# First-layer tiles of two squared-ReLU MLPs: pairs by quarters in seven products for eight, weights' sums on GpSimd

## Chip, cores and metric

The kernel runs on one core of one Trainium2 chip. The metric is the device time of one execution in microseconds (us). Before the change the median of three runs is 1992.46 us (1991.14 to 1993.85).

## What is computed

The input is x, 512 tokens by 1024 features, in float32. Two blocks follow each other: the first (latent attention beside a gated convolution, a gated feed-forward network, a gated embedding) and the second, which does this twice:

```python
for i in range(DEPTH_2):                       # DEPTH_2 = 2
    hn = _rmsnorm(h, mix_norm_g[i])
    h = h + (_retention if i % 2 == 0 else _chunk_attention)(hn, ...)
    h = h + _sqrelu_mlp(_rmsnorm(h, mlp_norm_g[i]), mlp_w1[i], mlp_w2[i])
return _rmsnorm(h, final_norm_g)

def _sqrelu_mlp(h, w1, w2):                    # w1: 1024 x 4096, w2: 4096 x 1024
    u = jax.nn.relu(h @ w1)
    return (u * u) @ w2
```

The change lies in `h @ w1` of the two MLPs, called MLP0 and MLP1 below.

## The kernel before

**Precision.** Every float32 operand of a product is split into a high part of TensorE's reduced float32 type and a low part, the rest. A product of a 128x128 weight tile with 128x512 activations is three matmuls into one bank of PSUM: high by high, low by high, high by low (`mm3`, L165 to L168). Activations lie features by tokens: eight `hn` pairs (`pair()`: high and low, 128x512 each) hold the normed input without the row factor, which the norm's spread `norm.r` brings in after the product.

**Weights.** `weights()` fetches one row of 128x128 tiles as a raw tile `wr` of 128x1024 (512 KB, one DMA on SyncE's queue, SP, L152; three buffers), ScalarE copies it to the high part `wh` (L129), VectorE subtracts to the low part `wl` (L113). Copy and subtraction are given a priority of 80 steps ahead (`HW`).

**An MLP** (`mlp`, from L969) goes in four groups. Each group has eight first-layer tiles (128 of the 4096 hidden features; eight tiles of depth by three matmuls are 24 matmuls of 512 columns), each followed by `square_relu`: VectorE multiplies the bank by `norm.r` (L107), takes max(t,0)*t (L975), and the split into a hidden pair follows (ScalarE L129, VectorE L113). Then come eight second-layer tiles (`m_w2`), each eight hidden pairs deep, which VectorE adds to the residual `xs` (L110). In group 0 the first two tiles are interleaved while the norm is being finished.

**Order.** TensorE's instructions run in the order in which the code writes them (`manual_schedule`, with generators that yield between pieces of a product). The order on the other engines' queues is set by a scheduler from the program and the priorities. Every queue runs in order: an instruction that waits holds up all behind it. Pools: 22 pairs, 8 temporaries of 128x512 (`tmp`), 8 banks of PSUM.

Of the kernel before, what the change touches and what calls it, by code (L numbers as in the profile page):

```python
# [7 lines left out]
F32 = mybir.dt.float32  # L8
# [6 lines left out]
P = 128  # L15
T = 512
# [45 lines left out]
def kernel(  # L62
# [32 lines left out]
    def f32(ap):  # L95
        return ap.bitcast(F32)
# [871 lines left out]

    def mlp(i, now, nxt):  # L969
        norm, hn = now.norm, now.hn  # L970

        def square_relu(hid, ps):
            t = tmp()
            mul(t, ps, norm.r)
            dve.scalar_tensor_tensor(out=t, in0=t, scalar=0.0, in1=t, op0=ALU.max, op1=ALU.mult)  # L975
            pr = pair()
            split(pr, t)
            hid.append(pr)

        def group(hid, grp):  # L980
            if grp == 0:

                two = [(bank(), weights(rows(m_w1, i * 32 + j))) for j in range(2)]
                yield from together([units(ps, w, K8, hn) for ps, w in two],
                                    [lambda ps=ps: norm.then(lambda: square_relu(hid, ps)) for ps, _ in two])
            for j in range(2 if grp == 0 else 0, 8):
                w = weights(rows(m_w1, i * 32 + grp * 8 + j))
                ps = bank()
                yield from units(ps, w, K8, hn)
                norm.then(lambda ps=ps: square_relu(hid, ps))  # L990
                yield

        for grp in range(4):
            hid = []
            gen = group(hid, grp)
# [4 lines left out]
            for mt in range(KT - 3 if ends else KT):  # L1000
# [432 lines left out]
```

## Time and profile before

| | |
|---|---|
| median of 3 runs | 1992.46 us (1991.14 to 1993.85) |
| the profiled execution, its own time | 1992.6 us |
| its span in the trace | 1990.8 us, 23850 instructions |
| TensorE matmuls (PE) busy | 1966.9 us, 99% |
| VectorE (DVE) busy | 1188.7 us, 60% |
| ScalarE (ACT) busy | 805.9 us, 40% |
| GpSimd (POOL) busy | 9.7 us |
| DMA | 185.31 MB, mean 93 GB/s |
| first-layer tiles of group 1 of MLP0 | 1134.70 to 1178.20 us |

The profiled execution's own time is 1.8 us above its span and 0.14 us above the median. Busy times sum the modelled durations; matmuls overlap each other, so that one matmul's duration is longer than the distance from its start to the next one's start. That distance, called spacing below, is a window's length divided by the matmuls that start in it.

### The profile page before, as it was taken

Reading aid. Unit: us, or ns where it says so; the run is one execution under the profiler, and the core shown is the slowest. Engines: PE = TensorE matmul, PEld = TensorE weight load, DVE = VectorE, ACT = ScalarE, POOL = GpSimd, SP = SyncE. Lnnn points to the kernel's source line nnn. Section 1 sums busy time; section 2 is a strip of 40 time slices with the busy share of each in tenths; the row PEclk is TensorE's granted clock in tenths of the full one; section 3 lists DMA queues with packets and bytes.
Section 4 is the critical chain, followed back from the end, with each engine's and each line's share of the span. In section 5 each row is a group of like instructions: output and inputs, shape, how many; then the busy total and the mean of one; then the engine's idle time right before and its main releaser. Section 6 shows DMA issues by size and latency. Waiting matters only on the chain.

```text
span 1990.8 us, 23850 instructions
## 1 busy us (share of the span) xinstructions
PE 1966.9 (99%) x9348; PEld 1643.8 (83%) x9348; DVE 1188.7 (60%) x2106; ACT 805.9 (40%) x1301; POOL 9.7 (0%) x21
## 2 busy tenths in 40 slices
PE   9999999999999999999999999999999999999998
PEld 7787888888888888888888888888888888888887
DVE  7878963343469665536565344455598975444354
ACT  5776542222245444233443222223476753222232
POOL 1000000000000000000000000000000000000000
PEclk9999999999999999999999999999999999999999
DMA  5122223232232222222222232222222223232321
GB/s 189 63 70 82 85 85 96 98 102 96 88 120 85 100 78 77 100 91 78 76 98 94 100 100 95 96 96 95 101 85 79 70 97 106 95 98 98 101 95 64
DMA packets 59041, 185.31 MB, mean 93 GB/s; under 512 B 6928, under 2 KB 10400, under 8 KB 58928
## 3 DMA queue, kind: packets, MB, share of 16 engines
q1 hardware_dynamic: 53936, 176.02, 26.2%
q10 hardware_dynamic: 4688, 7.40, 1.2%
q8 instruction: 73, 1.20, 0.3%
q0 software_dynamic: 304, 0.36, 0.1%
q14 instruction: 40, 0.33, 0.1%
HBM read 181.56 MB, written 2.20 MB: 92 GB/s over the span
## 4 chain that ended last, share of the span: by engine, by line
PE 89%; DVE 6%; ACT 3%; issue 1%; DMA 0%; POOLq 0%; POOL 0%; ACTq 0%; DVEq 0%
PE bank L166 29%; PE bank L168 29%; PE bank L167 29%; DVE wl L113 1%; PE bank L415 1%; PE bank L396 1%; ACT tmp L383 1%; ACT pair L129 1%; DVE pair L113 1%; DVE tmp L110 1%; DVE tmp L380 1%; DVE pt L113 1%; ACT wh L129 1%; PE bank L318 0%; DVE tmp L389 0%
## 5 line engine op out<-in xcount | busy, mean ns | idle before, releaser
L166 PE MATMUL bank<-pair,wh 128*128 128x512 f32 (+1 forms) x2550 | 978.8, 384 | 0.3 <-ACT pair L129 0.3
L168 PE MATMUL bank<-pair,wh 128*128 128x512 f32 (+1 forms) x2550 | 969.6, 380 | 0.5 <-DVE pair L113 0.3
L167 PE MATMUL bank<-pair,wl 128*128 128x512 f32 (+1 forms) x2550 | 968.5, 380 | 0.0
L129 ACT ACTIVATE wh<-wr 128x1024 fp32r<-128x1024 f32 (+5 forms) x355 | 353.7, 998 | 889.7 <-PE bank L168 643.3
L168 PEld LDWEIGHTS bank<-pair,wh 128*128 128x128 f32 x2550 | 480.0, 188 | 93.1 <-DVE pair L113 1.7
L166 PEld LDWEIGHTS bank<-pair,wh 128*128 128x128 f32 x2550 | 480.4, 188 | 87.8 <-ACT pair L129 0.9
L167 PEld LDWEIGHTS bank<-pair,wl 128*128 128x128 f32 x2550 | 480.6, 188 | 87.5 <-DVE wl L113 0.8
L113 DVE TENSOR_TENSOR wl<-wr,wh 128x1024 fp32r<-128x1024 f32 (+5 forms) x355 | 405.9, 1144 | 147.6 <-ACT wh L129 146.8
L107 DVE TENSOR_TENSOR tmp<-bank,rb 128x512 f32<-128x512 f32 (+1 forms) x140 | 94.4, 678 | 239.1 <-PE bank L168 235.3
L110 DVE TENSOR_TENSOR x<-x,bank 128x512 f32<-128x512 f32 (+1 forms) x99 | 66.2, 671 | 212.0 <-PE bank L168 211.9
L129 ACT ACTIVATE pair<-tmp 128x512 fp32r<-128x512 f32 (+1 forms) x188 | 118.6, 632 | 102.9 <-DVE tmp L975 28.3
L113 DVE TENSOR_TENSOR pair<-tmp,pair 128x512 fp32r<-128x512 f32 (+1 forms) x156 | 106.8, 687 | 12.3 <-ACT pair L129 11.3
L166 PE MATMUL bank<-wh,pair 128*128 128x512 f32 x200 | 79.2, 396 | 0.6 <-ACT tmp L129 0.6
L168 PE MATMUL bank<-wl,pair 128*128 128x512 f32 x200 | 78.0, 390 | 0.0
L167 PE MATMUL bank<-wh,pair 128*128 128x512 f32 x200 | 77.9, 389 | 0.0
L383 ACT ACTIVATE tmp<-tmp,small 128x512 f32<-128x512 f32 (+1 forms) x96 | 53.5, 558 | 33.9 <-DVE small L380 32.7
L110 DVE TENSOR_TENSOR tmp<-tmp 128x512 f32<-128x512 f32 (+1 forms) x90 | 57.0, 634 | 14.2 <-ACT tmp L268 13.5
L113 DVE TENSOR_TENSOR pt<-bank,pt 128x512 fp32r<-128x512 f32 (+1 forms) x96 | 42.8, 486 | 9.6 <-ACT pt L129 8.9
L975 DVE SCALAR_TENSOR_TENSOR tmp<-tmp 128x512 f32<-128x512 f32 x64 | 44.1, 692 | 2.0
L138 ACT ACTIVATE pair<-x,gn 128x512 fp32r<-128x512 f32 (+1 forms) x56 | 36.1, 654 | 22.2 <-DVE x L110 20.6
L166 PEld LDWEIGHTS bank<-wh,pair 128*128 128x128 f32 x200 | 37.6, 188 | 8.2 <-ACT tmp L129 1.0
L168 PEld LDWEIGHTS bank<-wl,pair 128*128 128x128 f32 x200 | 37.5, 188 | 8.0
(155 smaller groups left out, 1228.6 us busy)
## 6 DMA issues: line engine op xcount, KB each, us to landing
wr<-in_m_w_dram SPq DMA_DIRECT2D x128, 512.0 KB, 3.7
wr<-in_r_qkg_dram SPq DMA_DIRECT2D x32, 512.0 KB, 3.5
wr<-in_w_gate_dram SPq DMA_DIRECT2D x20, 512.0 KB, 3.5
wr<-in_w_up_dram SPq DMA_DIRECT2D x20, 512.0 KB, 3.4
wr<-in_w_down_dram SPq DMA_DIRECT2D x16, 512.0 KB, 3.4
wr<-in_r_v_dram SPq DMA_DIRECT2D x16, 512.0 KB, 3.5
wr<-in_r_out_dram SPq DMA_DIRECT2D x16, 512.0 KB, 3.6
wr<-in_a_qk_dram SPq DMA_DIRECT2D x16, 512.0 KB, 3.4
```

The costliest lines, as they stand in the source:

```text
L107: dve.tensor_tensor(out=out, in0=a, in1=b, op=ALU.mult)
L110: dve.tensor_tensor(out=out, in0=a, in1=b, op=ALU.add)
L113: return dve.tensor_tensor(out=out, in0=a, in1=b, op=ALU.subtract)
L129: act.activation(out, a, AF.Copy)
L138: act.activation(dst[:, 0, tok], src[:, tok], AF.Copy, scale=gain)
L166: pe.matmul(out, lhsT=ah, rhs=bh, start=start, stop=False)
L167: pe.matmul(out, lhsT=al, rhs=bh, start=False, stop=False)
L168: pe.matmul(out, lhsT=ah, rhs=bl, start=False, stop=stop)
L380: self.last = dve.tensor_tensor_reduce(out=s[:, :n], in0=ps[:, :n], in1=self.strip[:, T - n:T], scale=-self.scale, scalar=3.0e38, op0=ALU. ...
L383: act.activation(s[:, :n], s[:, :n], AF.Exp, bias=self.mx[:, col], scale=-1.0, accum_out=self.sm[:, col])
L396: pe.transpose(pt[:, j * P:(j + 1) * P], s[:, j * P:(j + 1) * P], ident)
L975: dve.scalar_tensor_tensor(out=t, in0=t, scalar=0.0, in1=t, op0=ALU.max, op1=ALU.mult)
```

## The change

A pair of neighbouring first-layer tiles j, k becomes one 2 by 2 block product: tile j or k, by depth halves `hn[0:4]` and `hn[4:8]`, by token halves of 256. Instead of eight quarter products it takes seven, each four depth tiles by three matmuls of 256 columns: 84 matmuls of 256 columns for 48 of 512. 13 pairs of each MLP are done so, 26 in all: tiles 6 and 7 of group 0, and all four pairs of groups 1 to 3. The operands of four of the seven products are sums of quarters:

- of activations, once in each MLP: `prepare(k)`, k = 0 to 3, called as the group-0 tiles 3, 4, 5 are written out and once more after tile 5. Each has two scaled copies on ScalarE, four sums of 128x256 on VectorE into a `qr` tile, then copy (ScalarE) and subtraction (VectorE) of 128x1024 into the pair `q0k`, `q1k`;
- of weights, for each pair: tile j is loaded as before; tile k is loaded raw into a `qr` tile (two buffers, the same two that `prepare` uses), GpSimd makes four sums of 128x512, and ScalarE and VectorE split these and the quarter a22 (five splits) into pairs, at a priority 150 steps ahead.

`square_relu` now takes max(bank,0)*norm.r in one VectorE instruction, squares on ScalarE, and splits; this for all 64 tiles. The eight hidden pairs are shared by the groups, and the first two second-layer tiles of each group are interleaved, with the last product of the group's last pair (`late`) between them. DMA volume is the same. Lines up to the class move by 1 to 3.

```diff
+HQ = 150
...
-    def split(dst, src, rows=slice(0, P)):
+    def split(dst, src, rows=slice(0, P), prompt_=False):
...
+        def prepare(self, k, gname):
+            hi, lo = (self.pool.tile([P, 4, T // 2], F32R, name=f"q{e}{k}", tag=f"q{e}{k}") for e in range(2))
+            p, q = tmp(), tmp()
+            act.activation(p, xs[k], AF.Copy, scale=g_(gname, k))
+            act.activation(q, xs[k + 4], AF.Copy, scale=g_(gname, k + 4))
+            (b11, b12), (b21, b22) = ([a[:, h] for h in HALVES] for a in (p, q))
+            t = self.pool.tile([P, 4, T // 2], F32, name="qr", tag="qr", bufs=2)
+            sub(t[:, 0, :], b12, b11)
+            sub(t[:, 2, :], b22, b12)
+            add(t[:, 1, :], t[:, 2, :], b11)
+            sub(t[:, 3, :], b21, t[:, 1, :])
+            copy(hi, t)
+            sub(lo, t, f32(hi))
+            self.sums.append((hi, lo))
...
+        def weights(self, src, j, k):
+            one = weight_tiles()
+            load_weights(one, rows(src, j), slice(0, 8 * P))
+            a = one[0]
+            b = self.pool.tile([P, 8 * P], F32, name="qr", tag="qr", bufs=2)
+            sp.dma_start(b, rows(src, k))
+            a11, a12, a21, a22 = a[:, :T], a[:, T:], b[:, :T], b[:, T:]
...
+            with tc.high_priority(offset=HQ):
+                t1, t2 = (self.pool.tile([P, T], F32, name="qs", tag="qs", bufs=2) for _ in range(2))
+                t3, t4 = tmp(), tmp()
+                total(t1, a21, a22, ALU.add)
+                s1 = parts(t1)
+                total(t2, t1, a11, ALU.subtract)
+                s2 = parts(t2)
+                total(t4, a12, t2, ALU.subtract)
+                s4 = parts(t4)
+                total(t3, a11, a21, ALU.subtract)
+                s3 = parts(t3)
+                a22 = parts(a22)
...
+        def two(self, src, j, k, end_j, end_k):
+            a11, a12, a22, s1, s2, s3, s4 = self.weights(src, j, k)
+            x, z = bank(), bank()
+            x0, x1, y0, z0 = x[:, HALVES[0]], x[:, HALVES[1]], z[:, HALVES[0]], z[:, HALVES[1]]
+            u, v = tmp(), tmp()[:, HALVES[0]]
+            yield from self.product(x0, a11, self.operand(0, 0), True)
+            copy(u[:, HALVES[0]], x0)
+            yield
+            yield from self.product(z0, s1, self.operand(None, 0), True)
+            copy(v, z0)
+            yield
+            yield from self.last()
+            yield from self.product(x0, s2, self.operand(None, 1))
+            copy(u[:, HALVES[1]], x0)
+            yield
+            yield from self.product(y0, a12, self.operand(1, 0))
+            yield
+            yield from self.product(z0, s4, self.operand(1, 1))
+            add(u, u, z)
+            end_j(u)
+            yield
+            yield from self.product(x0, s3, self.operand(None, 2))
+            add(x1, v, x0)
+            yield
+            def rest():
+                yield from self.product(x0, a22, self.operand(None, 3))
+                end_k(x)
+                yield
+            self.late = [rest()]
...
-            mul(t, ps, norm.r)
-            dve.scalar_tensor_tensor(out=t, in0=t, scalar=0.0, in1=t, op0=ALU.max, op1=ALU.mult)
...
+            dve.scalar_tensor_tensor(out=t, in0=ps, scalar=0.0, in1=norm.r, op0=ALU.max, op1=ALU.mult)
+            act.activation(t, t, AF.Square)
+            split(hid[j], t)
...
+            for j in range(6 if grp == 0 else 0, 8, 2):
+                yield from quarters.two(m_w1, r0 + j, r0 + j + 1, lambda u, j=j: square_relu(j, u),
+                                        lambda u, j=j: square_relu(j + 1, u))
```

The products of a pair are called P1 (a11), P2 (s1), P3 (s2), P4 (a12), P5 (s4), P6 (s3) and P7 (a22, `late`); u0 is the first copy out of x0, which P3 then writes on.

**VectorE, MLP0, from the result of tile 5 of group 0 on.** Before (`wl` are low parts of weights, the L113 `pair` rows those of hidden pairs):

```order
L107 TENSOR_TENSOR tmp_8940<-bank_8915,rb_8757 128x512
L975 SCALAR_TENSOR_TENSOR tmp_8940<-tmp_8940 128x512
L113 TENSOR_TENSOR wl_9017<-wr_9015,wh_9016 128x1024
L113 TENSOR_TENSOR pair_8943<-tmp_8940,pair_8943 128x512
L107 TENSOR_TENSOR tmp_8977<-bank_8952,rb_8757 128x512
L975 SCALAR_TENSOR_TENSOR tmp_8977<-tmp_8977 128x512
```

And now:

```order
L1088 SCALAR_TENSOR_TENSOR tmp_8935<-bank_8910,rb_8768 128x512
L114 TENSOR_TENSOR q11_8892<-qr_8897,q01_8891 128x1024
L114 TENSOR_TENSOR qr_8946<-tmp_8942 128x256
L114 TENSOR_TENSOR qr_8946<-tmp_8943,tmp_8942 128x256
L111 TENSOR_TENSOR qr_8946<-qr_8946,tmp_8942 128x256
L114 TENSOR_TENSOR pair_8669<-tmp_8935,pair_8669 128x512
L114 TENSOR_TENSOR qr_8946<-tmp_8943,qr_8946 128x256
L114 TENSOR_TENSOR qr_8959<-tmp_8955 128x256
L114 TENSOR_TENSOR qr_8959<-tmp_8956,tmp_8955 128x256
L111 TENSOR_TENSOR qr_8959<-qr_8959,tmp_8955 128x256
L114 TENSOR_TENSOR wl_9092<-wr_9090,wh_9091 128x1024
L114 TENSOR_TENSOR q12_8941<-qr_8946,q02_8940 128x1024
```

Eleven instructions now stand between the reading of tile 5's bank and the end of q12, the last reader of the `qr` tile 8946.

**SP's queue at the same place.** Before:

```order
L152 DMA wr_8909<-in_m_w1_dram 128x1024
L152 DMA wr_8946<-in_m_w1_dram 128x1024
L152 DMA wr_8983<-in_m_w2_dram 128x1024
L152 DMA wr_9015<-in_m_w2_dram 128x1024
L152 DMA wr_9047<-in_m_w2_dram 128x1024
L152 DMA wr_9079<-in_m_w2_dram 128x1024
```

And now (wr_8966 is tile 6, the first of the pair; qr_8972 is tile 7, its second, and takes the buffer of qr_8946):

```order
L155 DMA wr_8966<-in_m_w1_dram 128x1024
L155 DMA wr_9083<-in_m_w2_dram 128x1024
L155 DMA wr_9090<-in_m_w2_dram 128x1024
L155 DMA wr_9164<-in_m_w2_dram 128x1024
L155 DMA wr_9196<-in_m_w2_dram 128x1024
L279 DMA qr_8972<-in_m_w1_dram 128x1024
L279 DMA qr_9362<-in_m_w1_dram 128x1024
```

Tile 7 stood in the queue right behind tile 6; it now stands behind four transfers of second-layer weights, the last of which waits for wl_9092.

**ScalarE, MLP0, between the second and the third pair of group 2.** Before, weights and hidden pairs alternate:

```order
L129 ACTIVATE pair_9899<-tmp_9896 128x512
L129 ACTIVATE wh_10014<-wr_10013 128x1024
L129 ACTIVATE pair_9936<-tmp_9933 128x512
L129 ACTIVATE wh_10051<-wr_10050 128x1024
L129 ACTIVATE pair_9973<-tmp_9970 128x512
```

And now (pair_10412 is s1 of the third pair and takes the buffer of the second pair's s1; bank_10296 is x of the second pair, its first copy out is u0, its second the other half):

```order
L1089 ACTIVATE tmp_10247<-tmp_10247 128x512
L130 ACTIVATE pair_10412<-qs_10407 128x512
L130 ACTIVATE pair_8664<-tmp_10247 128x512
L130 ACTIVATE tmp_10298<-bank_10296 128x256
L130 ACTIVATE pair_10416<-qs_10408 128x512
L130 ACTIVATE tmp_10299<-bank_10297 128x256
L1089 ACTIVATE tmp_10338<-tmp_10338 128x512
L130 ACTIVATE tmp_10298<-bank_10296 128x256
```

The u0 copy of the second pair stands behind the split of the third pair's s1 and a hidden pair's copy; the first of these cannot start before the second pair's P2 has ended.

## Rows read from the trace of the kernel before

**Rows 1.** Page, span, PE's own row, and the chain by engine.

```profile
span 1990.8 us, 23850 instructions
PE 1966.9 (99%) x9348; PEld 1643.8 (83%) x9348; DVE 1188.7 (60%) x2106; ACT 805.9 (40%) x1301; POOL 9.7 (0%) x21
PE 89%; DVE 6%; ACT 3%; issue 1%; DMA 0%; POOLq 0%; POOL 0%; ACTq 0%; DVEq 0%
```

**Rows 2.** Windows, all engines, MLP0's group 1: window, length, then by engine.

```profile
1134.70:1178.20 43.50, 43.50 (x193) 36.03 (x192) 24.96 (x32) 13.61 (x16) 0.00 (x0) 1.00 0.30 95
```

**Rows 3.** Windows, PE, 256-column matmuls: window, length, busy (count), clock, DMA.

```profile
1961.79:1972.11 10.32, 10.32 (x88) 1.00 0.01 2
577.10:586.33 9.23, 9.23 (x79) 1.00 0.61 207
603.07:613.86 10.79, 10.63 (x89) 1.00 0.29 99
```

**Rows 4.** Timeline, then lines by form, PE, transposes of 128 columns.

```profile
1047.21 0.60 PE L281 MATMUL bank<-ident,tmp 128*128 128x128 f32 x4
L281 PE MATMUL bank<-ident,tmp 128*128 128x128 f32 x72 | 11.6, 279 | 4.8 <-DVE tmp L110 4.8
```

**Rows 5.** Timeline, DVE, MLP0's tiles 4 and 5; [idle before, releaser].

```profile
1069.42 0.69 DVE L107 TENSOR_TENSOR tmp<-bank,rb 128x512 f32<-128x512 f32 x1 [2.29 <-PE bank L168]
1070.14 0.69 DVE L975 SCALAR_TENSOR_TENSOR tmp<-tmp 128x512 f32<-128x512 f32 x1
1070.75 1.22 DVE L113 TENSOR_TENSOR wl<-wr,wh 128x1024 fp32r<-128x1024 f32 x1
1071.89 0.68 DVE L113 TENSOR_TENSOR pair<-tmp,pair 128x512 fp32r<-128x512 f32 x1
1074.86 0.69 DVE L107 TENSOR_TENSOR tmp<-bank,rb 128x512 f32<-128x512 f32 x1 [2.28 <-PE bank L168]
```

**Rows 6.** Lines by form: names, count | busy us, mean ns.

```profile
L113 DVE TENSOR_TENSOR wl<-wr,wh 128x1024 fp32r<-128x1024 f32 x298 | 364.2, 1223 | 142.3 <-ACT wh L129 141.6
L113 DVE TENSOR_TENSOR pair<-tmp,pair 128x512 fp32r<-128x512 f32 x140 | 95.9, 686 | 11.8 <-ACT pair L129 11.3
L975 DVE SCALAR_TENSOR_TENSOR tmp<-tmp 128x512 f32<-128x512 f32 x64 | 44.1, 692 | 2.0
L110 DVE TENSOR_TENSOR x<-x,tmp 128x256 f32<-128x256 f32 x32 | 12.8, 422 | 0.0
L129 ACT ACTIVATE wh<-wr 128x1024 fp32r<-128x1024 f32 x298 | 316.1, 1062 | 846.6 <-PE bank L168 625.7 <-issue 185.8 <-PE bank L167 34.2
L129 ACT ACTIVATE pair<-tmp 128x512 fp32r<-128x512 f32 x140 | 88.5, 633 | 100.4 <-DVE tmp L975 28.3 <-DVE tmp L1170 26.0 <-DVE tmp L110 16.2
L129 ACT ACTIVATE pt<-bank 128x256 fp32r<-128x256 f32 x24 | 9.2, 382 | 3.1 <-PE bank L396 2.9
L268 ACT ACTIVATE tmp<-x 128x512 f32<-128x512 f32 x46 | 27.9, 617 | 0.0
```

**Rows 7.** Lines by form, POOL: the only two-input GpSimd sums there are.

```profile
L1038 POOL TENSOR_TENSOR pair<-pair,tmp 128x256 f32<-128x256 f32 x2 | 1.4, 722 | 1006.4 <-ACT tmp L129 1006.4
```

**Rows 8.** DMA issues, MLP0: tile, count, KB each, median us from issue to landing.

```profile
wr<-in_m_w_dram SPq DMA_DIRECT2D x59, 512.0 KB, 3.7
```

**Rows 9.** Windows and timeline, PE, after waits of 2.36 and 1.98 us.

```profile
213.00:215.80 2.80, 0.44 (x4) 1.00 0.59 209
215.80:219.22 3.42, 3.42 (x15) 0.50 0.57 163
...
216.50 0.41 PE L167 MATMUL bank<-pair,wl 128*128 128x256 f32 x1
...
218.63 0.41 PE L168 MATMUL bank<-pair,wh 128*128 128x256 f32 x1
...
168.16 0.62 PE L396 MATMUL bank<-ident,tmp 128*128 128x128 f32 x3 [1.98 <-ACT tmp L387]
...
168.16:172.00 3.84, 3.84 (x19) 1.00 0.39 137
```

More of the change, by code (lines that the diff above doesn't have):

```diff
@@ L129, in copy @@
         act.activation(out, a, AF.Copy)
-    def split(dst, src, rows=slice(0, P)):
+    def split(dst, src, rows=slice(0, P), prompt_=False):
         copy(dst[rows, 0, :], src[rows, :])
-        sub(dst[rows, 1, :], src[rows, :], f32(dst[rows, 0, :]))
+        last = sub(dst[rows, 1, :], src[rows, :], f32(dst[rows, 0, :]))
+        if prompt_:
+            prompt.add(last.ins.name)
     def split_gain(src, gain, dst=None, tok=slice(0, T)):
@@ L239, in together, with __init__, operand, total @@
             yield
+    class Quarters:
+        def __init__(self, hn, pool):
+            self.hn, self.pool, self.sums, self.late = hn, pool, [], []
+        def prepare(self, k, gname):
[12 more added lines that the diff above has]
+            self.sums.append((hi, lo))
+        def operand(self, i, j):
+            if i is None:
+                return [(hi[:, j, :], lo[:, j, :]) for hi, lo in self.sums]
+            return [(a[:, 0, HALVES[j]], a[:, 1, HALVES[j]]) for a in self.hn[4 * i:4 * i + 4]]
+        def weights(self, src, j, k):
[5 more added lines that the diff above has]
+            a11, a12, a21, a22 = a[:, :T], a[:, T:], b[:, :T], b[:, T:]
+            def total(out, x, y, op):
+                nc.gpsimd.tensor_tensor(out=out, in0=x, in1=y, op=op)
+            def parts(src):
+                pr = pair()
+                split(pr, src, prompt_=True)
+                return pr[:, 0, :], pr[:, 1, :]
+            with tc.high_priority(offset=HQ):
[10 more added lines that the diff above has]
+                a22 = parts(a22)
+            hi, lo = one[1:]
+            return (hi[:, :T], lo[:, :T]), (hi[:, T:], lo[:, T:]), a22, s1, s2, s3, s4
+        def product(self, out, w, b, start=False):
+            hi, lo = w
+            for k, (bh, bl) in enumerate(b):
+                c = slice(k * P, (k + 1) * P)
+                for i, (x, y) in enumerate(((hi, bh), (lo, bh), (hi, bl))):
+                    pe.matmul(out, lhsT=x[:, c], rhs=y, start=start and k + i == 0, stop=k == 3 and i == 2,
+                              skip_group_check=True)
+                if k % 2 and k < 3:
+                    yield
+        def last(self):
+            for part in self.late:
+                yield from part
+            self.late = []
+        def two(self, src, j, k, end_j, end_k):
[25 more added lines that the diff above has]
+                end_k(x)
+                yield
+            self.late = [rest()]
@@ L970, in mlp, with square_relu, group @@
         norm, hn = now.norm, now.hn
-        def square_relu(hid, ps):
+        qpool = tc.tile_pool(name="qp", bufs=1, reuse_waits="tile")
+        quarters = Quarters(hn, qpool.__enter__())
+        hid = [pair() for _ in range(8)]
+        def square_relu(j, ps):
             t = tmp()
-            mul(t, ps, norm.r)
-            dve.scalar_tensor_tensor(out=t, in0=t, scalar=0.0, in1=t, op0=ALU.max, op1=ALU.mult)
[L976 to L980, printed above, removed]
+            dve.scalar_tensor_tensor(out=t, in0=ps, scalar=0.0, in1=norm.r, op0=ALU.max, op1=ALU.mult)
+            act.activation(t, t, AF.Square)
+            split(hid[j], t)
+        def group(grp):
+            r0 = i * 32 + grp * 8
             if grp == 0:
-                two = [(bank(), weights(rows(m_w1, i * 32 + j))) for j in range(2)]
+                two = [(bank(), weights(rows(m_w1, r0 + j))) for j in range(2)]
                 yield from together([units(ps, w, K8, hn) for ps, w in two],
[L985 to L991, printed above, removed]
+                                    [lambda j=j, ps=ps: norm.then(lambda: square_relu(j, ps))
+                                     for j, (ps, _) in enumerate(two)])
+                for j in range(2, 6):
+                    w = weights(rows(m_w1, r0 + j))
+                    ps = bank()
+                    yield from units(ps, w, K8, hn)
+                    norm.then(lambda j=j, ps=ps: square_relu(j, ps))
+                    if j > 2:
+                        quarters.prepare(j - 3, now.gname)
+                    yield
+                quarters.prepare(3, now.gname)
+            for j in range(6 if grp == 0 else 0, 8, 2):
+                yield from quarters.two(m_w1, r0 + j, r0 + j + 1, lambda u, j=j: square_relu(j, u),
+                                        lambda u, j=j: square_relu(j + 1, u))
         for grp in range(4):
-            hid = []
-            gen = group(hid, grp)
+            gen = group(grp)
             if grp == 0:
@@ L999, in mlp, with product, second_end @@
             ends = grp == 3 and nxt is None
-            for mt in range(KT - 3 if ends else KT):
+            def product(mt):
+                ws, ps = weights(rows(m_w2, i * KT + mt, grp * 8)), bank()
+                return units(ps, ws, K8, hid), lambda: second_end(mt, ps)
+            def second_end(mt, ps):
+                add(xs[mt], xs[mt], ps)
+                if ends:
+                    final.square(xs[mt])
+                elif grp == 3:
+                    nxt.take(mt)
+            first = together(*zip(*[product(mt) for mt in range(2)]))
+            pull(first, 2)
+            drain(quarters.last())
+            drain(first)
+            if grp == 3:
+                qpool.__exit__(None, None, None)
+            for mt in range(2, KT - 3 if ends else KT):
                 w = weights(rows(m_w2, i * KT + mt, grp * 8))
```

## Prediction

> **What bounds the kernel now.** The page comes first [rows 1]: TensorE (PE) is busy for 99% of the span and carries 89% of the chain that ended last. So time goes only where PE's own work gets shorter, and any wait that reaches PE is added in full. The second view is the table of windows for eight first-layer tiles [rows 2]: 192 matmuls of 512 columns start in 43.50 us, 0.2266 us apart, PE never pauses, and the other engines have room: VectorE is busy for 24.96 us, ScalarE for 13.61, GpSimd for none, and DMA runs at 0.30 of its time. What matters for the change is where this room lies. VectorE's timeline shows it [rows 5]: for each tile it waits 2.3 us for PE's bank and then works through four instructions in a row. Room of 2.3 us in 5.44 is all that can be filled before VectorE's queue starts to run late.
>
> The profiled execution took 1992.6 us, 0.14 above the median of the runs; the sum is made against 1992.6. Some 0.2% (4 us) is what a measurement of this kernel can tell from no change.
>
> **The products.** A pair takes 48 matmuls of 512 columns before, 48 x 0.2266 = 10.88 us, and 84 of 256 columns after. Three windows show 256-column matmuls without a pause [rows 3]. The counts include the two or three that were still running as the window opened, so 86, 77 and 86 start in 10.32, 9.23 and 10.79 us: 0.120, 0.120 and 0.1255 apart. I take 0.120, which two of three stretches show: 84 x 0.120 = 10.08, 0.80 less for each pair, 26 pairs: **-20.7 us**. At 0.1255 it would be only -8.7. The other end is the tightest spacing that any row shows: four transposes of 128 columns last 0.60 us together with 0.28 for one [rows 4], 0.32 / 3 = 0.107 apart; 84 x 0.107 = 8.99, -49 us.
>
> The Trainium skill ("TensorE: Matmul & The Clock Gate", section "Back-to-back issue gap") puts the gap of a lone matmul at N/2.4 + 2.5 ns at the full clock, 216 ns for 512 columns and 109 for 256; by it the term would be an estimate of -31 us. The windows disagree by 11 ns at either width [rows 2, 3], and the sum goes by them.
>
> **The first pair of each MLP.** Tiles 6 and 7 of group 0 come straight after tile 5. P1 needs only tile 6, loaded as before. P2 needs s1, a sum of two quarters of tile 7, and tile 7's transfer takes the `qr` buffer of the third activation block: it cannot start before VectorE's q12. In VectorE's queue q12 stands eleven instructions behind the reading of tile 5's bank, which can't start before PE ends tile 5. Their durations [rows 6]: the fused reading and the hidden pair 0.69 each, q11, wl and q12 1.22 each, seven sums of 128x256 at 0.42, together 7.98. Neighbours start some 0.08 before the last one's end (1070.75 + 1.22 against 1071.89 [rows 5]), 11 x 0.08 = 0.9 off, and I add 0.3 for a wait on ScalarE's copies: 7.4 us. Nothing lets VectorE begin early: in the 5.44 us from tile 4's result to tile 5's it now has a reading 0.69, q10 1.22, four sums 1.7, wl 1.22 and a hidden pair 0.69, 5.5 us for a gap of 5.44.
>
> Then tile 7 has to land, 3.7 us [rows 8]; GpSimd adds t1, ScalarE copies (0.63), VectorE subtracts (0.69 [rows 6]). GpSimd's price for 128x512 isn't in the trace; its only two sums are 128x256 at 0.72 us [rows 7]. So 0.72 (all fixed cost) to 1.44 (all per element); I take 1.3, nearer the upper end, since VectorE's two sizes, 0.42 and 0.69 [rows 6], are far from all fixed. With 0.3 for the handoffs P2 may start 7.4 + 3.7 + 1.3 + 0.63 + 0.69 + 0.3 = 14.0 us after tile 5's result. PE has only P1 meanwhile, 12 x 0.120 = 1.44, started 0.17 before that result: idle 14.0 + 0.17 - 1.44 = 12.7. The same order stands in MLP1: **+25.4 us**. Bounds: 10.9 each, if VectorE runs 1 us early and the sums are cheap; 15 each, if the transfer of second-layer weights issued 1.1 us ahead slows tile 7's.
>
> **The clock after it.** After a wait of 2.36 us the granted clock is 0.50 for 3.42 us, the lower of the two levels, 1.2 GHz [rows 9]; 256-column matmuls stand there (218.63 - 216.50) / 10 = 0.213 apart instead of 0.120, a loss of 3.42 x (1 - 0.120/0.213) = 1.5 us. After a wait of 1.98 us the clock stays at 1.00 [rows 9]. A wait of 12.7 us should lower it at least so long; 1.5 to 3.0, the middle, 2.2 in each MLP: **+4.4 us**.
>
> **The u0 copy.** In groups 1 to 3, P3 of a pair writes on the bank out of which u0 is copied. For the second and third pair of a group that copy stands on ScalarE behind the split of the next pair's s1, which takes the buffer that this pair's P2 reads. So from P2's result on: 0.25 for the handoffs, s1's copy 0.63, a hidden pair's 0.63, u0 0.38 [rows 6], 1.89 us, while PE has P7 of the pair before, 1.44. PE waits 0.45, 12 times in all: **+5.4 us**. Nothing, if ScalarE takes the copy early, is one end; 1 us each, if t1 comes late, is the other. The first and fourth pair have no such row ahead of the copy.
>
> **What costs nothing, and its cover.** Per pair VectorE has 1.22 + 5 x 0.69 + 0.69 + 0.42 + 2 x 1.38 = 8.5 us, ScalarE 1.06 + 5 x 0.63 + 3 x 0.38 + 2 x 1.25 = 7.9 (the square by the same kind, 0.62 [rows 6]), GpSimd 5.2, beside 10.1 to 10.5 of PE. That is 84% of VectorE's time where it was 57% [rows 2]: a fifth more on VectorE and PE waits. The loop through the two raw buffers (a22's split, transfer, t1 to t3, splits) takes some 9.6 us, under the pair's 10.5. The second-layer tiles (8 x 5.44 us) let the next group's first weights come early. The late product at a group's end lies inside two interleaved tiles, and hid[7] is ready some 2.9 us after it while 8 us of other products remain. `square_relu`'s move of one instruction from VectorE to ScalarE is off PE's path, DMA volume is unchanged.
>
> **Sum.** -20.7 + 25.4 + 4.4 + 5.4 = +14.5: 1992.6 + 14.5 = **2007 us**. The low ends of the last three (21.8, 3.0, 0) give 1997, the high ends (30, 6, 12) 2020.
>
> **Rivals.**
> *VectorE and GpSimd in each other's way.* In before they hardly run together; the two GpSimd sums [rows 7] ran beside VectorE work that read a bank, so no row prices it. Here GpSimd works for half of each pair, while 6.7 of VectorE's 8.5 us read two operands of SBUF. If a GpSimd sum then takes twice 1.3, the loop of the raw buffers grows by four sums, 5.2 us, to 14.8, past the pair's 10.5; the two spare buffers carry the first two pairs of a group and the third waits some 3.5 instead of 0.45: 6 groups x 3.05 = 18, and 1.3 for each first pair: +21, 2028 us. For it: the loop has no more than 1 us of room. Against it: nothing in before shows it. It begins to cost at about 1.3 times the price. The Trainium skill ("GPSIMD Engine Reference", section "8. Key points") says that GpSimd shares its interfaces to SBUF with VectorE and contends with instructions that have two SBUF inputs; no run here shows it yet. Chance 0.17.
> *The first pair doesn't wait* (the other side). If the raw buffer were free, or VectorE's queue ran far ahead, tile 7 would land under tiles 4 and 5, and the sum is 1992.6 - 20.7 + 5.4 = 1977 us. For it: DMA is at 0.30 [rows 2], and SP's queue holds nothing else that must be waited for. Against it: the order of the queue and 5.5 us of work in 5.44. It decides where wait and clock fall under (20.7 - 5.4) / 2 = 7.6 us in each MLP; half of my chain is fixed by transfer, sum and split alone (6.6 us). Chance 0.08.
> *The products run closer.* At 0.107 the products give -49, waits and clock stay (u0 waits 0.6, since P7 covers less): about 1980. It turns the sign under 0.113. For it: the transposes' spacing at 128 columns [rows 4]. Against it: three long stretches at 0.120 or more [rows 3]. Chance 0.09, a third of it within 0.2%.
>
> **How the numbers follow.** My case has 0.66, its own range 1997 to 2020. Faster: 0.08 + 0.06 = 0.14. Same (1988.5 to 1996.4): 0.03 and 0.05 of my case, where the first pair waits some 5 us less than the chain says, 0.08. Slower: 0.61 + 0.17 = 0.78. The range goes from 1992, which takes in that lower edge, to 2030, past the rival with GpSimd; left out are the two faster cases and the worst of the contention, under 0.2.
>
> **What would show it.** Right: in each MLP one gap on PE of 11 to 15 us after twelve 256-column matmuls behind tile 5, released by VectorE's split of s1, the transfer of tile 7 issued at q12's end, then a stretch at 0.50; 256-column spacing of 0.120; 12 gaps of 0.3 to 0.6 us released by the u0 copy. Wrong: no such gap; spacing under 0.113; GpSimd sums above 1.7 us and gaps of several us at third pairs; or VectorE rather than PE without pause in groups 1 to 3.

## The result and the profile after

| | before | after |
|---|---|---|
| median | 1991.80 us (4 runs, 1991.06 to 1993.85) | 2018.72 us (4 runs, 2017.05 to 2021.19) |
| ratio | | 1.0134, 95% interval 1.0117 to 1.0152 |
| profiled execution, its span | 1990.8 us | 2015.2 us |

The change costs 27 us; 14.5 were forecast. The time is inside the range, the sign is right, the size is short by half. The page's first two lines, which answer to [rows 1], show that PE now pauses: two points of busy share fewer, and work on GpSimd (POOL) that was not there.

```profile
span 2015.2 us, 26327 instructions
PE 1952.5 (97%) x10284; PEld 1673.0 (83%) x10284; DVE 1300.4 (65%) x2238; ACT 924.6 (46%) x1571; POOL 176.2 (9%) x125
```

The view of PE's waits of the kernel after says where (instruction, what it waited for: us in total, times, longest). L310 are the quarter products. The first row is s1 of the two first pairs; the second is a copy out of x0 (`tmp` out of a bank), 12 times: ten times u0 before P3, twice the second copy before P6; the third is the low part of s1.

```profile
PE bank L310 <- ACT pair L130: 26.6, 2, 13.5
PE bank L310 <- ACT tmp L130: 10.3, 12, 1.7
...
PE bank L310 <- DVE pair L114: 1.3, 2, 0.7
```

The timeline of the kernel after shows the chain of the first of these waits, engine by engine. Tile 5's bank is read from 1073.26 us on; q12 ends at 1081.16 (7.9 us later), SP issues tile 7's transfer at once, GpSimd can begin 4.6 us later, and then come the sum, the copy and the subtraction. P2's first matmul starts when the copy is done, after PE has stood idle for 13.14 us; its second waits another 0.65 us for the subtraction. The row at 1082.62 is q13, VectorE's last work for the activation sums: it is done at 1083.85, before GpSimd has begun.

```profile
1073.26 0.69 DVE L1088 SCALAR_TENSOR_TENSOR tmp<-bank,rb 128x512 f32<-128x512 f32 x1 [0.19 <-PE bank L171]
...
1079.94 1.22 DVE L114 TENSOR_TENSOR q<-qr,q 128x1024 fp32r<-128x1024 f32 x1
...
1081.23 3.01 SPq L279 DMA_DIRECT2D qr<-in_m_w_dram  x2
...
1082.62 1.23 DVE L114 TENSOR_TENSOR q<-qr,q 128x1024 fp32r<-128x1024 f32 x1 [1.12 <-ACT q L130]
1085.82 1.25 POOL L283 TENSOR_TENSOR qs<-qr 128x512 f32<-128x512 f32 x1 [1045.66 <-DMA qr<-in_m_w_dram]
1087.11 0.63 ACT L130 ACTIVATE pair<-qs 128x512 fp32r<-128x512 f32 x1 [4.52 <-POOL qs L283]
1087.77 1.20 DVE L114 TENSOR_TENSOR pair<-qs,pair 128x512 fp32r<-128x512 f32 x1 [3.93 <-ACT pair L130]
...
1087.79 0.58 PE L310 MATMUL bank<-q,pair 128*128 128x256 f32 x1 [13.14 <-ACT pair L130]
...
1089.02 0.58 PE L310 MATMUL bank<-q,pair 128*128 128x256 f32 x1 [0.65 <-DVE pair L114]
```

Five windows of the kernel after follow (window, length, PE busy and count, PEld, DVE, ACT, POOL, clock, DMA): pairs without a wait, the clock after the long wait (three windows), and the first-layer part of MLP0's group 1, which answers to [rows 2].

```profile
1143.00:1155.00 12.00, 12.00 (x103) 12.00 (x102) 7.16 (x10) 6.69 (x12) 1.30 (x1) 1.00 0.01 2
1087.79:1090.00 2.21, 1.56 (x5) 1.26 (x6) 2.06 (x2) 0.90 (x2) 2.13 (x2) 0.50 0.00 0
1090.00:1092.00 2.00, 2.00 (x12) 2.00 (x11) 1.85 (x2) 0.79 (x2) 2.00 (x3) 0.50 0.00 0
1092.00:1094.00 2.00, 2.00 (x16) 1.85 (x16) 1.85 (x3) 1.64 (x4) 1.50 (x1) 0.98 0.47 119
1142.74:1185.08 42.34, 40.75 (x331) 39.87 (x330) 32.78 (x42) 24.21 (x45) 13.65 (x8) 1.00 0.30 92
```

In the first, 100 matmuls of 256 columns start in 12.00 us (three were running), 0.119 from one start to the next, where [rows 3] had 0.120. In the last, VectorE is busy for 32.8 us of 42.3.

Distances from start to start add up over both MLPs like this: 26 pairs of 84 matmuls at the normal spacing save 22.6 us; the first pairs lose 29.7; the pauses for copies out of x0 lose 13.7 (18 of them, six too short for the wait table), and 1.9 more because the second matmul behind each pause starts 0.22 us after the first, at a granted clock of 1.00; 25 matmuls of 256 columns in the stretches at 0.50 start 0.21 apart and lose 2.3; small rests 1.1. That is +26.1. Before the MLPs the two profiled executions differ by 1.6 the other way, where [rows 9] had its spell at 0.50, so the spans differ by 24.4.

### The profile page after: what moved, and what is told of

Read it like the earlier page. It is cut to its first block, busy times and chain, and to the rows that moved or that the text cites. A ratio compares the mean times of both kernels' runs of the same rounds, so it can differ in the third digit from the quotient of the medians.

```text
span 2015.2 us, 26327 instructions
## 1 busy us (share of the span) xinstructions
PE 1952.5 (97%) x10284; PEld 1673.0 (83%) x10284; DVE 1300.4 (65%) x2238; ACT 924.6 (46%) x1571; POOL 176.2 (9%) x125
## 4 chain that ended last, share of the span: by engine, by line
issue 57%; PE 30%; DVE 6%; ACT 3%; POOL 2%; DMA 2%; SPq 0%; POOLq 0%; ACTq 0%; DVEq 0%
PE bank L169 7%; PE bank L171 7%; PE bank L170 7%; PE bank L310 6%; DVE wl L114 2%; DMA qr<-in_m_w_dram 1%; DVE pair L114 1%; POOL tmp L283 1%; ACT pair L130 1%; DVE tmp L111 1%; PE bank L526 1%; POOL qs L283 1%; ACT wh L130 1%; DVE tmp L500 0%; DVE tmp L491 0%
## 5 line engine op out<-in xcount | busy, mean ns | idle before, releaser
L169 PE MATMUL bank<-pair,wh 128*128 128x512 f32 (+1 forms) x2134 | 816.4, 383 | 0.2 <-ACT pair L130 0.2
L171 PE MATMUL bank<-pair,wh 128*128 128x512 f32 (+1 forms) x2134 | 807.6, 378 | 0.5 <-DVE pair L114 0.3
L170 PE MATMUL bank<-pair,wl 128*128 128x512 f32 (+1 forms) x2134 | 806.4, 378 | 0.0
L171 PEld LDWEIGHTS bank<-pair,wh 128*128 128x128 f32 x2134 | 401.4, 188 | 77.0 <-DVE pair L114 1.7
L169 PEld LDWEIGHTS bank<-pair,wh 128*128 128x128 f32 x2134 | 401.9, 188 | 70.9 <-ACT pair L130 0.8
L170 PEld LDWEIGHTS bank<-pair,wl 128*128 128x128 f32 x2134 | 402.0, 188 | 70.4 <-DVE wl L114 0.5
L114 DVE TENSOR_TENSOR pair<-tmp,pair 128x512 fp32r<-128x512 f32 (+1 forms) x208 | 171.2, 830 | 63.7 <-ACT pair L130 60.7
L310 PE MATMUL bank<-q,pair 128*128 128x256 f32 x1248 | 166.4, 287 | 38.8 <-ACT pair L130 26.6
L310 PEld LDWEIGHTS bank<-q,pair 128*128 128x128 f32 x1248 | 157.0, 192 | 44.2 <-ACT pair L130 27.1
L283 POOL TENSOR_TENSOR qs<-qr 128x512 f32<-128x512 f32 x26 | 40.9, 1573 | 1478.0 <-DMA qr<-in_m_w_dram 1478.0
L108 DVE TENSOR_TENSOR tmp<-bank,rb 128x512 f32<-128x512 f32 (+1 forms) x76 | 50.2, 666 | 103.9 <-PE bank L171 101.3
L310 PE MATMUL bank<-pair,wh 128*128 128x256 f32 x416 | 83.0, 283 | 0.0
L310 PEld LDWEIGHTS bank<-pair,wh 128*128 128x128 f32 x416 | 67.8, 190 | 0.8 <-ACT tmp L130 0.2
```

Of the source, the lines that this page charges most:

```text
L169: pe.matmul(out, lhsT=ah, rhs=bh, start=start, stop=False)
L170: pe.matmul(out, lhsT=al, rhs=bh, start=False, stop=False)
L171: pe.matmul(out, lhsT=ah, rhs=bl, start=False, stop=stop)
L283: nc.gpsimd.tensor_tensor(out=out, in0=x, in1=y, op=op)
L310: pe.matmul(out, lhsT=x[:, c], rhs=y, start=start and k + i == 0, stop=k == 3 and i == 2, skip_group_check=True)
```

## The experiments

**Group 0 without a pair.**

```diff
-                for j in range(2, 6):
+                for j in range(2, 8):
...
-            for j in range(6 if grp == 0 else 0, 8, 2):
+            for j in range(8 if grp == 0 else 0, 8, 2):
```

> Edit: group 0 of each MLP keeps eight ordinary tiles; 24 pairs instead of 26, all in groups 1 to 3; prepare stays behind tiles 3, 4, 5 and 5. Theory A (the time went into the first pair: 24.65 us for its first 72 matmuls of 256 columns where 8.6 would do, 16 us in each MLP, waiting for tile 7's transfer): both waits of 13.4 us go, no half clock in group 0, two pairs' gain of 0.9 is given up: 2018.7 - 32 + 1.8 = 1988 us. Rival B (VectorE is behind with prepare's work whatever stands there, so the wait moves to the first pair of group 1 or to the second-layer tiles): above 2005 us with a wait of 5 us or more elsewhere.

Measured: 1987.51 us, ratio to before 0.9978 (0.9968 to 0.9987). Both long waits are gone, and none of 5 us came elsewhere: the first pairs cost 31 us, and without them the change is a small gain. 9.1 us of P3 waits stay.

**The transfer alone.**

```diff
-            t = self.pool.tile([P, 4, T // 2], F32, name="qr", tag="qr", bufs=2)
+            t = f32(pair()).rearrange("p e (h t) -> p (e h) t", h=2)
```

> Edit: prepare writes its four sums into a free activation pair instead of the raw-weight buffers, so that tile 7's transfer waits for nothing in group 0 (it then stands before the last transfers of the retention layer). Theory A1 (the transfer behind q12 is what costs): the waits of 13.4 us go almost wholly: 1988 to 1992 us. Theory A2 (VectorE's backlog is the larger part: s1 and the last two activation blocks still stand behind tile 5's reading, and P2 needs all four blocks): P2 begins some 6 us late and its last two depth tiles come 2 to 4 us later, a wait of 8 to 9 us in each MLP instead of 14.5: 2007 to 2010 us.

Measured: 2018.08 us, ratio 1.0128 (1.0113 to 1.0143): no gain. The waits of PE in this kernel:

```profile
PE bank L310 <- ACT pair L130: 13.3, 2, 6.7
...
PE bank L310 <- DVE q L114: 5.4, 4, 2.2
...
PE bank L310 <- ACT q L130: 2.7, 4, 0.8
```

s1 comes 6.6 us late instead of 13.3, as theory A2 had it, but then P2 creeps: its third and fourth depth tile wait for q12 and q13, which VectorE reaches after the five weight splits. P2's last wait ends 17 us after P1's start; in the kernel after it was 16. So theory A1 falls, and A2's time (2007 to 2010) was missed too. VectorE's timeline in this kernel, from the five splits to q13, shows why:

```profile
1083.77 1.29 DVE L114 TENSOR_TENSOR pair<-qs,pair 128x512 fp32r<-128x512 f32 x2
1084.98 2.38 DVE L114 TENSOR_TENSOR pair<-tmp,pair 128x512 fp32r<-128x512 f32 x2
1087.28 0.68 DVE L114 TENSOR_TENSOR pair<-qr,pair 128x512 fp32r<-128x512 f32 x1
...
1090.89 1.22 DVE L114 TENSOR_TENSOR q<-pair,q 128x1024 fp32r<-128x1024 f32 x1 [1.12 <-ACT q L130]
```

Here q13 ends 16.9 us after P1's start; in the kernel after it ended 10.8 us after it, since the splits were not ready before tile 7 had landed. An early tile 7 lets its splits, 4.2 us of them, go ahead of q12 and q13. What took the gain away is thus VectorE's order as well as its load; q12 and q13 ahead of the splits was not tried.

**And one block less in the backlog.** prepare(j - 2) behind tiles 2 to 5, on top of the last kernel:

```diff
-                    if j > 2:
-                        quarters.prepare(j - 3, now.gname)
+                    quarters.prepare(j - 2, now.gname)
...
-                quarters.prepare(3, now.gname)
```

> Edit on own_scratch: prepare is called after tiles 2, 3, 4 and 5, one block each, instead of 3, 4, 5 and 5. Theory A2 (with the transfer out of the way the first pair waits for VectorE's backlog alone, which ends 16 to 17 us after P1's start in own_scratch): one block's work (2.9 us) and its collisions are taken out of the backlog; P2 ends some 10 to 11 us after P1's start, 5 to 6 us less in each MLP: 2006 to 2008 us. Rival (the wait belongs to GpSimd or to the order of the splits, not to how much VectorE has to do): no gain, 2015 us or more.

Measured: 2010.40 us, ratio 1.0084 (1.0069 to 1.0100); 7.7 less than own_scratch, 4 in each MLP where 5 to 6 were expected. P2's last wait ends 14 us after P1's start. The direction is A2's, the size is below it; the five splits still stand ahead of q13.

**u0 ahead of the splits.**

```diff
-            copy(u[:, HALVES[0]], x0)
+            with tc.high_priority(offset=HQ * 2): copy(u[:, HALVES[0]], x0)
```

> Edit: the first copy out of x0 (u0) gets a priority of 300 steps ahead, so that on ScalarE it stands ahead of the next pair's s1 split. Theory: the 12 waits of P3 on that copy (10.3 us of idle, 0.86 each) go: 2018.7 - 11 = 2007 to 2009 us. Rival: ScalarE then holds the splits of s3 and a22 behind the copy, which waits for P1, and the wait comes back at the later products: 2015 us or more.

Measured: 2019.05 us, ratio 1.0134 (1.0119 to 1.0150): no gain, but not by the rival's way. PE's waits in this kernel:

```profile
PE bank L310 <- ACT pair L130: 26.8, 2, 13.5
PE bank L310 <- DVE bank L111: 7.7, 11, 1.0
...
PE bank L310 <- ACT tmp L130: 2.4, 5, 0.7
```

The u0 waits fell from 10.3 to 2.4, and 7.7 us came on VectorE's sum `add(x1, v, x0)`: VectorE is as late as ScalarE was. One such sum is the second pair's in group 1 (the last row below); PE waits 0.7 us for it. In front of it VectorE works without a pause beside GpSimd:

```profile
1161.52 1.42 DVE L114 TENSOR_TENSOR pair<-tmp,pair 128x512 fp32r<-128x512 f32 x1 [1.36 <-ACT pair L130]
1162.34 1.75 POOL L283 TENSOR_TENSOR tmp<-wr,qs 128x512 f32<-128x512 f32 x1
1162.86 0.68 DVE L111 TENSOR_TENSOR tmp<-tmp,bank 128x512 f32<-128x512 f32 x1
1163.45 1.72 DVE L114 TENSOR_TENSOR wl<-wr,wh 128x1024 fp32r<-128x1024 f32 x1
1165.09 1.77 DVE L1088 SCALAR_TENSOR_TENSOR tmp<-tmp,rb 128x512 f32<-128x512 f32 x1
1166.78 0.42 DVE L111 TENSOR_TENSOR bank<-tmp,bank 128x256 f32<-128x256 f32 x1
```

The three instructions that read two SBUF tiles take 4.9 us together; by their durations in the kernel before [rows 6] they would take 2.6. At this place the slowing is 2.3 us, more than the wait. The sum at 1162.86, which reads a bank, keeps its 0.68.

**Without the sums.**

```diff
-                total(t1, a21, a22, ALU.add)
-                s1 = parts(t1)
+                s1 = parts(a21)
...
-                total(t3, a11, a21, ALU.subtract)
-                s3 = parts(t3)
+                s3 = parts(a21)
```

> Left out: the four sums of weight quarters on GpSimd; the five splits take raw quarters instead. Theory C (GpSimd beside VectorE makes both slower, 2.06 us for a weight subtraction instead of 1.22, and this is why u0 waits 0.86 instead of 0.45): subtractions go back to 1.22 and 0.69, the u0 waits fall to some 0.45, and the first wait is 1.3 shorter: 2018.7 - 5 - 3 = 2011 us. Rival D (u0 waits for the order on ScalarE alone): u0 waits stay at 0.8 or more, 2016 us.

This kernel leaves out the four sums of weight quarters. Measured: 1999.51 us, ratio 1.0033 (1.0022 to 1.0045), 19 us below the kernel after where 8 were expected. Not one P3 wait is left, and the first pairs wait 24.1 us instead of 27.9. The window of the same work, and VectorE's groups in it (count | busy us, mean ns), without sums:

```profile
1143.31:1183.24 39.93, 39.93 (x331) 39.67 (x330) 28.15 (x42) 25.21 (x45) 0.00 (x0) 1.00 0.36 109
```

```profile
L114 DVE TENSOR_TENSOR wl<-wr,wh 128x1024 fp32r<-128x1024 f32 x5 | 6.1, 1226 | 3.5 <-ACT wh L130 3.5
...
L114 DVE TENSOR_TENSOR pair<-tmp,pair 128x512 fp32r<-128x512 f32 x6 | 4.1, 689 | 3.4 <-ACT pair L130 3.4
```

And the same two groups in the kernel after, from 1142.74 to 1185.08 us:

```profile
L114 DVE TENSOR_TENSOR pair<-tmp,pair 128x512 fp32r<-128x512 f32 x12 | 10.8, 910 | 3.6 <-ACT pair L130 3.3
L114 DVE TENSOR_TENSOR wl<-wr,wh 128x1024 fp32r<-128x1024 f32 x5 | 7.7, 1540 | 3.6 <-ACT wh L130 3.6
```

The same subtractions take 910 ns instead of 689 and 1540 instead of 1226 beside GpSimd: VectorE's 42 instructions take 32.8 us instead of 28.2. GpSimd suffers too, as the next view shows. The run took away the contention, the time of the sums themselves and their place in GpSimd's queue, so it does not say which of the three PE waits for.

The timeline of the kernel after at the fourth pair of group 1 shows the wait of 1.2 us from the other side:

```profile
1170.45 1.47 POOL L283 TENSOR_TENSOR qs<-qr 128x512 f32<-128x512 f32 x1 [5.41 <-DMA qr<-in_m_w_dram]
1171.87 2.28 POOL L283 TENSOR_TENSOR tmp<-wr,qs 128x512 f32<-128x512 f32 x1
1174.11 1.74 POOL L283 TENSOR_TENSOR tmp<-wr,qr 128x512 f32<-128x512 f32 x1
1174.19 0.63 ACT L130 ACTIVATE pair<-tmp 128x512 fp32r<-128x512 f32 x1 [3.19 <-POOL tmp L283]
1175.88 0.63 ACT L130 ACTIVATE pair<-tmp 128x512 fp32r<-128x512 f32 x1 [1.06 <-POOL tmp L283]
1176.42 0.61 ACT L130 ACTIVATE pair<-qr 128x512 fp32r<-128x512 f32 x1
1176.94 0.61 ACT L1089 ACTIVATE tmp<-tmp 128x512 f32<-128x512 f32 x1
1177.46 0.36 ACT L130 ACTIVATE tmp<-bank 128x256 f32<-128x256 f32 x1
...
1177.87 0.51 PE L310 MATMUL bank<-q,pair 128*128 128x256 f32 x2 [1.23 <-ACT tmp L130]
```

u0 (the 128x256 copy) stands behind the splits of its own pair's s4, s3 and a22, and ScalarE waits there for GpSimd's last two sums, 2.28 and 1.74 us long where the one that stood alone took 1.25. Two things make these sums late. The three sums shown take 5.5 us instead of 3 x 1.25, 1.7 more, for a wait of 1.2. And the first of them is t1 of the next group's first pair: it stands in GpSimd's queue ahead of this pair's t4 and t3, and GpSimd stood idle 5.41 us for its transfer. (It is the next pair's: the t4 at 1171.87 uses a t2, the last of which ran at 1163.29, and a t2 comes behind its own t1.) No run changed that order alone.

**Raw buffers free earlier, two ways, on g0_plain.**

```diff
                 total(t1, a21, a22, ALU.add)
                 s1 = parts(t1)
+                total(t3, a11, a21, ALU.subtract)
+                a22 = parts(a22)
                 total(t2, t1, a11, ALU.subtract)
...
-                total(t3, a11, a21, ALU.subtract)
                 s3 = parts(t3)
-                a22 = parts(a22)
```

> Edit on g0_plain: GpSimd's sums in the order t1, t3, t2, t4 and a22 split right behind t3, so that the raw buffer of the second tile is free two sums earlier. Theory L (the waits of P3, 9.1 us in g0_plain, come from the loop through the two raw buffers: a22's split, transfer, sums beside VectorE at up to 2.28 us, s3's split on ScalarE, behind which u0 stands): the next transfer but one starts some 3 us earlier, the waits at third and fourth pairs go: 1987.5 - 9 = 1977 to 1980 us. Rival V (VectorE is full: 32.8 us of 42 in a group, with bursts): the waits stay at 6 us or more, 1984 us or above.

```diff
-            b = self.pool.tile([P, 8 * P], F32, name="qr", tag="qr", bufs=2)
+            b = self.pool.tile([P, 8 * P], F32, name="qr", tag="qr", bufs=3)
...
-                t1, t2 = (self.pool.tile([P, T], F32, name="qs", tag="qs", bufs=2) for _ in range(2))
+                t1, t2 = tmp(), tmp()
```

> Edit on g0_plain: three raw buffers instead of two; t1 and t2 take temporaries to make room. Theory L: transfers run one more pair ahead, GpSimd is never late, the waits of P3 go: 1977 to 1980 us. Rival V: waits of 6 us or more stay, 1984 us or above. A third way: temporaries run out (t1 to t4, u, v and a square for each pair, of 8) and new waits come: above 1988 us.

Measured: 2000.36 us (1.0041, 1.0028 to 1.0055) and 2015.86 us (1.0120, 1.0107 to 1.0134): 13 and 28 us above g0_plain. Theory L falls. The first fits the rival's bound (1984 or above), the second the third way's (above 1988), but neither had said that the time would grow so far. In g0_order PE's waits in the quarter products are 17.1 us where g0_plain has 9.1, and after three of its six waits of 1.9 us the granted clock is 0.50 for some 3.4 us (1241.80 to 1245.20 is one stretch). By the 1.5 us that such a stretch costs in the prediction's working that is 4.5 more, an estimate; with the 8.0 of the waits it makes 12.5 of the 13. With the new order GpSimd itself waits for VectorE; these are its two groups with the longest waits of that kind:

```profile
L283 POOL TENSOR_TENSOR qs<-qs,wr 128x512 f32<-128x512 f32 x24 | 40.4, 1685 | 76.0 <-DVE pair L114 73.1 <-DMA wr<-in_m_w_dram 2.4
...
L283 POOL TENSOR_TENSOR qs<-qr 128x512 f32<-128x512 f32 x24 | 36.4, 1516 | 1442.6 <-DMA qr<-in_m_w_dram 1386.9 <-DVE pair L114 45.3 <-DVE tmp L1088 7.0
```

With three raw buffers the collisions on VectorE grow: the splits of a22 take 1637 ns each where g0_plain has 1050, and PE waits for splits, 20.6 us in 18 waits, which g0_plain does not have.

```profile
L114 DVE TENSOR_TENSOR pair<-qr,pair 128x512 fp32r<-128x512 f32 x24 | 39.3, 1637 | 0.0
```

```profile
PE bank L310 <- DVE pair L114: 20.6, 18, 1.6
```

How much of the 28 us the temporaries cost (the third way) was not tried apart.

**The sums on VectorE, on g0_plain.**

```diff
-                nc.gpsimd.tensor_tensor(out=out, in0=x, in1=y, op=op)
+                dve.tensor_tensor(out=out, in0=x, in1=y, op=op)
```

> Edit on g0_plain: the four sums of weight quarters on VectorE instead of GpSimd. No engine then slows VectorE, whose work for a group's pairs is 28.2 us (as in no_sums) plus 16 x 0.69 = 39 us of PE's 40. Theory V (what counts is VectorE's total): waits of some 1 us for each pair, 24 in all: 1990 to 2005 us. Rival C (the contention is the larger cost): under 1985 us.

Measured: 2005.39 us, ratio 1.0069 (1.0056 to 1.0083), 18 above g0_plain. GpSimd with its collisions is the better place of the two. But the time is not lost in 24 waits of 1 us, as theory V had it. There are six, one in each group, and the granted clock is 0.50 for some 3 us or more after each:

```profile
PE bank L310 <- DVE bank L111: 22.9, 6, 4.1
```

In group 1 the sum that PE waits for comes at 1151.93, behind the weight sums and the five splits, which have the higher priority, and at the head of these VectorE stood idle for 1.80 us until the next pair's tile had landed. So this run shows again what the order of a queue costs; it does not show that VectorE's total is too large.

**The square alone.**

```diff
-            mul(t, ps, norm.r)
-            dve.scalar_tensor_tensor(out=t, in0=t, scalar=0.0, in1=t, op0=ALU.max, op1=ALU.mult)
+            dve.scalar_tensor_tensor(out=t, in0=ps, scalar=0.0, in1=norm.r, op0=ALU.max, op1=ALU.mult)
+            act.activation(t, t, AF.Square)
```

> The kernel before with nothing but the fused reading and the square on ScalarE. Expected: no change beyond 0.2%, 1990 to 1994 us, since both engines stood idle there. Rival: a gain of 2 us or more, which would then have to be taken off the gain put down to the products in g0_plain.

Measured: 1992.75 us, ratio 1.0005 (0.9996 to 1.0014). Nothing, as expected.

**Room between the pairs, on g0_plain.**

```diff
+            for j in (0, 2, 3, 5, 6):
+                if j in (2, 5):
...
+                    pull(tile_units, 2)
+                    yield from quarters.last()
+                    yield from tile_units
+                    square_relu(j, ps)
```

> Edit on g0_plain: three pairs for each of groups 1 to 3 instead of four, with an ordinary tile after the first and after the second (pair, tile, pair, tile, pair); 18 pairs in all. Theory V (VectorE's total beside GpSimd is what makes P3 wait, not the latency of a single pair's chain): an ordinary tile takes 5.4 us of PE and 2.6 of VectorE, so VectorE catches up and all waits of P3 go; left are 18 x 0.88 = 15.8 us of gain less some 3 us for the 30 changes of width: 1992 - 13 = 1979 us, 8 below g0_plain. Rival L (each pair's own chain of transfer, sums and splits is too long): the third pair still waits and six pairs' gain is lost: 1987 us or more.

Measured: 1995.34 us, ratio 1.0014 (1.0006 to 1.0023): slower than g0_plain, against theory V. ScalarE's timeline at the second pair of group 1 shows what theory V left out:

```profile
1142.71 1.06 ACT L130 ACTIVATE wh<-wr 128x1024 fp32r<-128x1024 f32 x1 [1.95 <-PE bank L171]
1143.68 1.14 ACT L130 ACTIVATE pair<-tmp 128x512 fp32r<-128x512 f32 x2
...
1146.80 0.36 ACT L130 ACTIVATE tmp<-bank 128x256 f32<-128x256 f32 x1
```

A weight copy stands in the queue until PE has ended the ordinary tile, with ScalarE idle for 1.95 us, and the pair's splits, ready or not, stand behind it, and u0 behind those. PE waits 14.0 us in 12 waits, for the order of a queue and not for work.

**Both.** The priority of u0 on spaced_pairs and, as the control, on g0_plain (edits as above).

> Edit: u0_early's priority on spaced_pairs. In spaced_pairs u0 stands on ScalarE behind its own pair's splits, and these behind a weight copy that waits for the ordinary tile's matmuls (1142.71 us, then 4.1 us of copies before u0). In u0_early alone the gain was eaten by VectorE, late with the sum that the late product waits for. Theory W (two queues one behind the other: ScalarE's order first, VectorE's load beside GpSimd second; spacing gives VectorE the room that u0_early lacked): both waits go, 1992 - 13 = 1979 to 1982 us. Rival (VectorE stays late even with room, or the splits behind u0 come late in turn): 1988 us or more, with waits on VectorE's sum or on the splits.

> Edit: u0_early's priority on g0_plain, 24 pairs without ordinary tiles between. Theory W (VectorE has no room in four pairs in a row beside GpSimd): the waits move from u0 to VectorE's sum, 5 to 8 us of them in all, and the time stays at g0_plain's: 1984 to 1989 us, not under spaced_u0_early. Rival (ScalarE's order is the whole cause): waits fall under 3 us and six pairs more than in spaced_u0_early give 4 us more: 1979 us or less.

Measured: 1983.13 us, ratio 0.9956 (0.9943 to 0.9970), and 1987.11 us, ratio 0.9978 (0.9969 to 0.9987). In the first, PE's waits in the quarter products fell to one row:

```profile
PE bank L310 <- ACT tmp L130: 3.2, 6, 0.5
```

In the control they moved to VectorE's sum, as theory W has it:

```profile
PE bank L310 <- DVE bank L111: 8.2, 12, 0.8
...
PE bank L310 <- ACT tmp L130: 3.1, 5, 0.7
```

Two queues stand one behind the other. With u0 early and room between the pairs, 18 pairs bring more than 24 without, and spaced_u0_early beats both kernels, by 9 us the one before. It ends 1 us above the expectation's range; six waits of 0.5 us, 3.2 in all, stay.

## Why the prediction was right, and where it was short

- **The products** (-20.7): right, -22.6; the spacing was 0.119 instead of 0.120. The rival at 0.107 is out. The third window of [rows 3] was not without a pause, as the text says (PE was busy for 10.63 us of 10.79), so its 0.1255 contains an idle 0.16 us. The gap of a lone matmul that the Trainium skill gives ("TensorE: Matmul & The Clock Gate", section "Back-to-back issue gap"), 109 ns for 256 columns, doesn't hold in these windows: 119.
- **The first pair** (+25.4): right in mechanism, place and count, 29.7 measured. Of its chain q12 ended after 7.9 us instead of 7.4, tile 7 landed in 4.6 instead of 3.7 (second-layer weights were issued 1.2 us ahead of it, the upper bound's case), GpSimd took 1.25 instead of 1.3, and s1's subtraction 1.20 instead of 0.69, beside GpSimd's second sum; the wait came in two parts, 13.1 us for ScalarE's copy and 0.65 for this subtraction. What it did not see: once tile 7 lands early, its splits go ahead of q12 and q13 on VectorE, so taking the transfer away gains nothing. The text's other-side rival ("If the raw buffer were free, or VectorE's queue ran far ahead") is wrong in its first half, by own_scratch; the second half alone was not tried.
- **The clock** (+4.4): right in kind, too large. The granted clock was 0.50 when PE began again after each long wait, and for some 4 us from then on; the 25 matmuls spaced at the lower clock lose 2.3. Some 1 us more, an estimate, lies within the 29.7: in each P2 the second matmul starts 0.58 us after the first, its wait taken off, and the third 0.38 after the second.
- **The u0 copy** (+5.4): this is the step that failed, 15.6 with the two pauses at P6 and the slow matmul behind each pause. "The first and fourth pair have no such row ahead of the copy" was wrong for the fourth: it waits longest in four of the six groups, 1.2 us in MLP0's group 1 and up to 1.9 from start to start, behind its own pair's splits and GpSimd's sums; the rule looked only at the next pair's s1. In group 3 of each MLP it does not wait, and the third pair has the pause at P6, which the sum had not at all. The second pairs' pauses are 0.09 us of idle time instead of 0.45. The rival with GpSimd named a cause that enlarged it, and gave it 0.17 as a case of its own, at twice the price everywhere. It came at part of the price (1.25 to 2.28 us for a sum, 0.69 to 0.91 for a split), and the time stayed in the range of the likeliest case: no_sums has no such wait at all. Of the sign that was set for it, sums above 1.7 us came (two of the four groups have a mean of 1.7), the gaps of several us at third pairs did not.
- **Cover**: "a fifth more on VectorE and PE waits" was near: 28.2 us became 32.8 in group 1, 16% more, and in u0_early VectorE's sum is what PE waits for. That the square's move costs nothing was right.

It is in part luck that the total is no further off: the products and the clock came out better than their terms, by 4 us together, the first pairs and the copies worse, by 14. What stays open is how the P3 waits divide between the sums' own time, the slowing of both engines and the place of the next pair's t1 in GpSimd's queue, since no run took away one without the others, and why the new order of g0_order made the waits longer.

## What to carry over

Saving matmuls on a saturated TensorE pays only where the operands' preparation fits on every other engine with contention counted in; here the saving was 22.6 us, and two late pairs and copies at the wrong place of a queue took 45. Put the first use of prepared operands a whole phase behind their preparation (g0_plain): what is taken from one late chain, another queue can give back (own_scratch). An instruction for the next pair that waits for a transfer, put ahead by its priority, holds up the present pair's work behind it. When a copy that frees a bank stands behind work that waits, move it forward, and then look which queue is late next: over g0_plain only priority and room together paid.

## What the hardware showed unexpectedly

VectorE and GpSimd slow each other down when VectorE reads two SBUF tiles: a 128x512 subtraction went from 0.69 us to a mean of 0.91, a 128x1024 one from 1.23 to 1.54, a GpSimd sum from 1.25 alone to as much as 2.28. A VectorE sum with a bank among its inputs kept its 0.68 beside GpSimd (u0_early, 1162.86). The Trainium skill ("GPSIMD Engine Reference", section "8. Key points") says, without a figure, that GpSimd contends with VectorE instructions with two SBUF inputs, and these rows agree. That a third raw buffer, with the temporaries for t1 and t2, made the kernel 28 us slower (g0_three_raw) was not expected by theory L or V.
